# The chain of a chunked RWKV7 recurrence cut from three products a chunk to two, and the tensor engine put into written order

## The chip, the cores and the metric

The kernel runs on one core of one Trainium2 chip. The metric is the device time of one execution in microseconds, lower is better.

The core has a tensor engine (PE) that multiplies, three engines for elementwise work, VectorE (DVE), ScalarE (ACT) and GpSimd (POOL), and SyncE (SP), on whose queue the DMA transfers of this kernel are started. Each runs its own list of instructions in the order of that list, and engines wait for each other by semaphores. Products are accumulated in PSUM, from which VectorE or ScalarE copies them out.

## The reference

One decoder block: a combined input projection, a gated spatial unit (SGU) and an RWKV7 recurrence side by side, an output projection with residual, and cross-attention over 256 memory tokens. Sequence length is 1024, model width 1024; the recurrence has 8 heads of 64. What matters here is the recurrence, a linear one with a state S of 64x64 a head:

```python
def rwkv7_step(state, inp):
    r, w, k, v, a, bb = inp
    sa = jnp.einsum('bhvk,bhk->bhv', state, a)
    state = state * w[:, :, None, :] + sa[..., None] * bb[:, :, None, :] + v[..., None] * k[:, :, None, :]
    y = jnp.einsum('bhvk,bhk->bhv', state, r)
    return state, y
...
h = h + jnp.concatenate([y_sgu, y_rwkv], axis=-1) @ w_out[l]
h = h + mem_cross_attention(h, mem, ln_x_g[l], ln_mem_g[l], w_q[l], w_kv[l], w_o[l])
```

## The kernel before, in words

**Chunks.** The 1024 steps are cut into 16 chunks of 64. Two heads make a pair and share the 128 partitions, so there are 4 pairs, and each pair's sequence is worked in two halves of 8 chunks: 8 halves, counted by n from 0 to 7. Within a chunk the recurrence becomes products. Four masked products of the chunk's factors with each other ("grams"), the inverse of a triangular matrix, and the state of the chunk before give the chunk's output and the next state.

**The stages of a half.**
- `elementwise` (L577 to L636) makes the decay factors. Its products are the decay product (L583, L584), sums (L608) and the bonus (L635).
- `grams` (L656 to L705) makes the grams of each quarter (4 chunks) as 16 products into two PSUM accumulators `co`, empties them with VectorE (L661 to L666), and inverts 16x16 diagonal blocks with VectorE (L673 to L679). The inverse goes through memory (`t_img`, started on SP at L680) and comes back as `t16`.
- `turn` transposes the values and the update factors of a quarter: `avt` (L696, copied by ScalarE at L698) and `bkt` (L702, L703).
- `solve` makes the full 64x64 inverse triangles, `tt`, from the 16x16 blocks in four steps. Each step is one or two batches of 16 products of 64x64 (L717, `pair_mm`) into `cb` or `co`.
- `serial` runs the chunks one after the other. Per chunk it has three products into `us`: `us[0]` applies the factors `ra` to the state (L766); VectorE adds `akv` to one part of it and puts it on the diagonal of `abdiag` (two 64x64 adds, L768); `us[1]` applies the triangle `tt` (L775); ScalarE copies the result into `avt` (L776); `us[2]` makes the state's update (L781), and VectorE adds it to the decayed state, two 64x64 (L787). ScalarE also makes the decayed state (L772) and the chunk's first output part (L778).
- `outputs` (L799, L801) adds the grams' part of the output once per quarter; `finish` normalises a half (L809 to L819, with a power on GpSimd inside `rsqrt_small`, L152 and L153), transposes it (L823) and stores it to `y_scr` (L828).

**Accumulators.** PSUM tiles named `co` exist twice, `cb` once. Decay products, bonus, grams and the transposes of `turn` all use the two `co`.

**Dense work in between.** The input projection, later the output projection, is a long list of dense products. `mm3` issues three products of 128x512 for each step (L177 to L179), since each operand is split into a high and a low part (helper L156, L157; weights are fetched at L161). The function `drive` (L896) runs for n from −2 to 7 and weaves the stages of neighbouring halves: beside the chunks of half n it writes the outputs and end of n − 1, the grams, transposes and solve of n + 1, the elementwise work of n + 2, and 32 or so dense steps. The tables `D_*` give each step a cost and `W_*` a stretch of the half in which its steps are due; `D_HOP` gives the distance between the products of a chunk.

**What sets the order.** The written order is only a proposal in this kernel: a scheduler of the language takes the program and decides each engine's list itself, the tensor engine's included (`with nullcontext():` ahead of the loop over n). Buffers of a rotating tile come free in turn.

Of the kernel before, what the change touches and what calls it, by code (L numbers as in the profile page):

```python
# [18 lines left out]
P = 128  # L19
# [3 lines left out]
C = 64  # L23
# [12 lines left out]
W_S = (0.72, 1.0)  # L36
# [4 lines left out]
D_HOP = (1.2, 0.95, 1.3)  # L41
# [4 lines left out]
D_S = (1.3, 1.3, 2.2, 1.3)  # L46
# [36 lines left out]
def tile_hybrid_block(ctx: ExitStack, tc: tile.TileContext, x, xT, mem, memT, cst_d, vec_d, w_sv, w_blk, w2_d, a2_d,  # L83
# [17 lines left out]
    def cb_ps():  # L101
        return psB.tile([P, 512], F32, name="cb")
# [8 lines left out]
    def cs_(n):  # L111
        o, w = CST[n]
        return cst[:, o:o + w]
# [342 lines left out]
    with tc.tile_pool(name="rw", bufs=1) as rw:  # L456
# [6 lines left out]
        ab_d = [rw.tile([P, P], F32, name=f"abdiag{i}") for i in range(2)]  # L463
        z_buf = [rw.tile([P, NC, C], F32, name=f"zz{i}") for i in range(2)]
        for t in st_d + ab_d + z_buf:
            nc.gpsimd.memset(t, 0.0)
# [240 lines left out]
        def solve(i):  # L707

            u, qs = halves_u[i], quarters[2 * i:2 * i + 2]
            t16 = u["t16"]  # L710
# [30 lines left out]
            u.update(tt=tt, akv=akv)  # L741
            yield

        def serial(i):

            u = halves_u[i]
            ra, dc, tt, akv = u["ra"], u["dc"], u["tt"], u["akv"]
            u["y"] = ytok = rw.tile([P, 4, P], F32, name="ytok", bufs=2)
            for c in range(NC):
# [7 lines left out]
                s_old, s_new, ab = st_d[n % 2], st_d[(n + 1) % 2], ab_d[n % 2]  # L757
                us = psC.tile([P, 3, P], F32, name="us")
                yc = ytok[R[c % 2], c // 2, :]
                if first:  # L760
                    nc.gpsimd.memset(yc, 0.0)
                    for hh in range(2):
                        nc.vector.tensor_copy(out=ab[R[hh], R[hh]], in_=akv[R[hh], c, :])
                else:

                    nc.tensor.matmul(us[:, 0, :], ra[:, c, :, :], s_old, start=True, stop=True)  # L766
                    for hh in range(2):
                        nc.vector.tensor_tensor(out=ab[R[hh], R[hh]], in0=us[R[1], 0, R[hh]], in1=akv[R[hh], c, :],  # L768
                                                op=ALU.add)
# [9 lines left out]
                yield  # L779
                if not last:  # L780
                    nc.tensor.matmul(us[:, 2, :], bkt[:, cq, :], avt[:, cq, :], start=True, stop=True)  # L781
                    for h2 in R:
                        if first:
# [419 lines left out]
```

## Time and profile before

| | us |
|---|---|
| median of 3 runs | 953.71 (952.59 to 954.79) |
| profiled execution | 952.35 |
| its span | 950.6 |
| tensor engine busy | 906.8 (95% of the span) |
| VectorE busy | 593.5 (62%) |
| ScalarE busy | 390.5 (41%) |
| GpSimd busy | 50.5 (5%) |

The span is read in parts. SGU and the first projection lie ahead of 243 us; the recurrence runs from there to 664 us; behind it follow the rest of the output projection and the attention. A "busy" tensor engine may still be filling or draining its pipeline: a dense product shows 0.39 us but the next one starts 0.23 us behind it, so prices are taken from the distance of starts. The chain that ended last goes through the tensor engine for 78% of the span and through VectorE for 13%.

### The profile page before, as it was taken

How to read it: one execution, taken by the hardware profiler on the slowest of the kernel's cores; microseconds unless marked ns; L12 is line 12 of the kernel's file. 1: busy time of each engine (PE TensorE's matmuls, PEld its weight loads, DVE VectorE, ACT ScalarE, POOL GpSimd, SP SyncE). 2: the span in 40 equal slices, each digit the busy share in tenths (PEclk: the TensorE clock that was granted, in tenths of full speed). 3: DMA queues.
4: the chain of work that ended last, by engine and by line, in shares of the span. 5: the costliest groups of instructions: out<-in, count | busy, mean ns of one | idle time of the engine just before them, and what ended most of it. 6: DMA issues, size and time to landing. Idle time of an engine off the chain costs nothing.

```text
span 950.6 us, 16113 instructions
## 1 busy us (share of the span) xinstructions
PE 906.8 (95%) x6236; PEld 728.1 (77%) x6236; DVE 593.5 (62%) x1375; ACT 390.5 (41%) x818; POOL 50.5 (5%) x115
## 2 busy tenths in 40 slices
PE   6989999999999999898989999999799999999996
PEld 6978888888777777676767677677698778888885
DVE  5867233334585878686868789867587664444333
ACT  6763222224442525252616272534266553333222
POOL 0001000012000000000000000000000000000000
PEclk9999999999999999999999999999999999999999
DMA  8862011113122112121111084425462400000001
GB/s 314 264 216 89 23 67 67 67 68 111 40 55 44 37 26 60 26 59 26 48 35 49 24 240 113 115 52 151 143 212 70 136 6 2 26 26 26 26 32 45
DMA packets 86092, 76.86 MB, mean 81 GB/s; under 512 B 38272, under 2 KB 58752, under 8 KB 86016
## 3 DMA queue, kind: packets, MB, share of 16 engines
q1 hardware_dynamic: 84864, 73.73, 24.9%
q10 hardware_dynamic: 1152, 2.10, 0.6%
q8 instruction: 49, 0.80, 0.4%
q14 instruction: 27, 0.22, 0.1%
HBM read 62.17 MB, written 13.64 MB: 80 GB/s over the span
## 4 chain that ended last, share of the span: by engine, by line
PE 78%; DVE 13%; issue 3%; DMA 2%; POOL 2%; ACT 1%; POOLq 0%; SPq 0%; DVEq 0%; ACTq 0%
PE mm L177 21%; PE mm L179 20%; PE mm L178 20%; PE cb L717 3%; PE us L766 2%; PE us L775 2%; PE yps L799 2%; PE us L781 1%; POOL grs L153 1%; DVE gr L666 1%; PE co L717 1%; DVE stdiag L787 1%; DMA w_raw<-in_w_sv 1%; DVE cs L592 1%; PE co L432 1%
## 5 line engine op out<-in xcount | busy, mean ns | idle before, releaser
L177 PE MATMUL mm<-xh,w_hi 128*128 128x512 f32 x400 | 167.2, 418 | 0.0
L179 PE MATMUL mm<-xh,w_lo 128*128 128x512 f32 x400 | 159.8, 400 | 0.0
L178 PE MATMUL mm<-xl,w_hi 128*128 128x512 f32 x400 | 159.5, 399 | 0.0
L157 DVE TENSOR_TENSOR w_lo<-w_raw,w_hi 128x512 fp32r<-128x512 f32 x115 | 78.7, 686 | 63.9 <-ACT w_hi L156 61.4
L156 ACT CAST w_hi<-w_raw 128x512 fp32r<-128x512 f32 x115 | 70.8, 617 | 91.4 <-PE mm L178 75.8
L179 PEld LDWEIGHTS mm<-xh,w_lo 128*128 128x128 f32 x400 | 75.8, 190 | 14.8 <-issue 0.2
L177 PEld LDWEIGHTS mm<-xh,w_hi 128*128 128x128 f32 x400 | 76.0, 190 | 12.9 <-issue 1.0
L178 PEld LDWEIGHTS mm<-xl,w_hi 128*128 128x128 f32 x400 | 76.2, 190 | 12.5 <-issue 0.5
L177 PE MATMUL mm<-wo,w_hi 128*128 128x512 f32 x128 | 54.2, 424 | 0.0
L776 ACT COPY avt<-us 64x128 f32<-64x128 f32 x64 | 16.6, 259 | 90.1 <-PE us L775 89.8
L178 PE MATMUL mm<-wo,w_hi 128*128 128x512 f32 x128 | 52.4, 409 | 0.0
L179 PE MATMUL mm<-wo,w_lo 128*128 128x512 f32 x128 | 51.8, 404 | 0.0
L177 PE MATMUL mm<-vp_h,p_hi 128*128 128x512 f32 x128 | 51.3, 401 | 0.0
L179 PE MATMUL mm<-kp_h,w_lo 128*128 128x512 f32 x128 | 50.1, 391 | 0.0
L177 PE MATMUL mm<-kp_h,w_hi 128*128 128x512 f32 x128 | 50.0, 391 | 0.0
L179 PE MATMUL mm<-vp_h,p_lo 128*128 128x512 f32 x128 | 50.0, 390 | 0.0
L178 PE MATMUL mm<-vp_l,p_hi 128*128 128x512 f32 x128 | 49.9, 390 | 0.0
L178 PE MATMUL mm<-kp_l,w_hi 128*128 128x512 f32 x128 | 49.9, 389 | 0.0
L787 DVE SCALAR_TENSOR_TENSOR stdiag<-us,dc,sd 64x64 f32<-64x64 f32 x112 | 31.6, 283 | 21.9 <-PE us L781 19.4
L772 ACT ACTIVATE sd<-stdiag,dc 128x128 f32<-128x128 f32 x56 | 22.4, 399 | 40.7 <-DVE stdiag L787 37.1
L1040 DVE TENSOR_REDUCE mx<-mm 128x2 f32<-128x512 f32 x16 | 11.1, 691 | 41.8 <-PE mm L179 41.8
L499 ACT ACTIVATE t<-mm,vec 128x512 f32<-128x512 f32 x34 | 23.3, 684 | 33.7 <-PE mm L179 32.7
(272 smaller groups left out, 2029.1 us busy)
## 6 DMA issues: line engine op xcount, KB each, us to landing
w_raw<-in_w_blk SPq DMA_DIRECT2D x50, 256.0 KB, 2.5
w_raw<-y_scr SPq DMA_DIRECT2D x32, 256.0 KB, 3.3
w_raw<-in_w_kv SPq DMA_DIRECT2D x17, 256.0 KB, 3.9
xr<-in_xT SPq DMA_DIRECT2D x8, 512.0 KB, 5.7
w_raw<-in_w_out SPq DMA_DIRECT2D x16, 256.0 KB, 2.8
h_all<-in_x SPq DMA_DIRECT2D x16, 256.0 KB, 4.5
pr<-in_w_qT SPq DMA_DIRECT2D x8, 512.0 KB, 4.4
w_raw<-in_w_o SPq DMA_DIRECT2D x16, 256.0 KB, 2.6
```

What stands on the lines that cost most here:

```text
L156: nc.scalar.copy(out=hi, in_=src)
L157: (eng or nc.vector).tensor_tensor(out=lo, in0=src, in1=hi.bitcast(F32), op=ALU.subtract)
L177: nc.tensor.matmul(ps, lh, rh, start=first, stop=False)
L178: nc.tensor.matmul(ps, lh, rl, start=False, stop=False)
L179: nc.tensor.matmul(ps, ll, rh, start=False, stop=last)
L499: nc.scalar.activation(out=t1[:, 1:HT + 1], in_=ps, func=AF.Copy, scale=vc("mu", b))
L717: nc.tensor.matmul(ps[R[hh], c, :], fl(hh, c), fr(hh, c), start=True, stop=True)
L766: nc.tensor.matmul(us[:, 0, :], ra[:, c, :, :], s_old, start=True, stop=True)
L772: nc.scalar.activation(out=sd, in_=s_old, func=AF.Copy, scale=dcc)
L775: nc.tensor.matmul(us[:, 1, :], tt[:, c - c % 2:c - c % 2 + 2, :], ab, start=True, stop=True)
L787: nc.vector.scalar_tensor_tensor(out=s_new[h2, h2], in0=us[h2, 2, h2], scalar=dcc[h2], in1=sd[h2, h2], op0=ALU.mult, op1=ALU.add)
L799: nc.tensor.matmul(yps[R[c % 2], o:o + 64], gr[:, c, hh, :], avt[:, c, R[hh]], start=True, stop=True)
```

## The change

It has three parts.

**Two products a chunk.** Write A for the `a` part of `ra`, T for the triangle. The three products of a chunk compute T(A S + akv). The new `solve` computes T A and T akv for all 8 chunks of a half ahead of the chain, in a fifth step: A is transposed with the identity (16 products, `at`), T A is made (16 products) and copied by ScalarE over the `a` part of `ra`, T akv is made (16 products) and copied by ScalarE into `avt` in four parts. `serial` is left with `us[0]`, one VectorE add of 64x128 straight into `avt`, and the state's update. The second product, its ScalarE copy and `abdiag` are gone. `tt` and `akv` now have one buffer each instead of two.

**The tables.** `D_HOP` has two entries, `D_S` five; the solve's steps are due from 0.66 instead of 0.72 of a half; the gate of the first outputs of a half goes from 12 to 8 steps, since a chunk has two steps now instead of three.

**The tensor engine's order.** `with nullcontext()` becomes `with tc.manual_schedule(engines={PE})`: the tensor engine's list in the loop over n is the written order. The other engines are still ordered by the scheduler.

```diff
-W_S = (0.72, 1.0)
+W_S = (0.66, 1.0)
-D_HOP = (1.2, 0.95, 1.3)
+D_HOP = (1.0, 1.35)
-D_S = (1.3, 1.3, 2.2, 1.3)
+D_S = (2.2, 1.3, 2.2, 1.3, 2.2)
...
-            t16 = u["t16"]
+            t16, ra = u["t16"], u["ra"]
...
-            tt = rw.tile([P, NC, C], F32, name="tt", bufs=2)
+            tt = rw.tile([P, NC, C], F32, name="tt")
...
-            akv = rw.tile([P, NC, C], F32, name="akv", bufs=2)
+            akv = rw.tile([P, NC, C], F32, name="akv")
+            at = rw.tile([P, NC, C], F32, name="at")
...
+            pa = pair_mm(co_ps(), lambda hh, c: ra[R[hh], c, 1, :], lambda hh, c: ident[R[hh], R[hh]])
+            nc.scalar.copy(out=at, in_=pa)
...
-            u.update(tt=tt, akv=akv)
+            yield
+            ps = pair_mm(cb_ps(), lambda hh, c: at[R[hh], c, :], lambda hh, c: tt[R[hh], c, :])
+            pa = pair_mm(co_ps(), lambda hh, c: tt[R[hh], c, :], lambda hh, c: akv[R[hh], c, :])
+            nc.scalar.copy(out=ra[:, :, 1, :], in_=ps)
+            for j in range(2):
+                for hh in range(2):
+                    nc.scalar.copy(out=qs[j]["avt"][R[0], :, R[hh]], in_=pa[R[hh], QC * j:QC * j + QC, :])
...
-                us = psC.tile([P, 3, P], F32, name="us")
+                us = psC.tile([P, 2, P], F32, name="us")
...
                     nc.tensor.matmul(us[:, 0, :], ra[:, c, :, :], s_old, start=True, stop=True)
-                    for hh in range(2):
-                        nc.vector.tensor_tensor(out=ab[R[hh], R[hh]], in0=us[R[1], 0, R[hh]], in1=akv[R[hh], c, :],
-                                                op=ALU.add)
+                    nc.vector.tensor_tensor(out=avt[R[0], cq, :], in0=us[R[1], 0, :], in1=avt[R[0], cq, :], op=ALU.add)
...
-                nc.tensor.matmul(us[:, 1, :], tt[:, c - c % 2:c - c % 2 + 2, :], ab, start=True, stop=True)
-                nc.scalar.copy(out=avt[R[0], cq, :], in_=us[R[c % 2], 1, :])
...
-                    nc.tensor.matmul(us[:, 2, :], bkt[:, cq, :], avt[:, cq, :], start=True, stop=True)
+                    nc.tensor.matmul(us[:, 1, :], bkt[:, cq, :], avt[:, cq, :], start=True, stop=True)
...
-                    (ok(n), lambda: outputs(2 * n), D_Y, W_Y0, 12),
+                    (ok(n), lambda: outputs(2 * n), D_Y, W_Y0, 8),
...
-        with nullcontext():
+        with tc.manual_schedule(engines={mybir.EngineType.PE}):
```

In the new program most line numbers of the recurrence differ by one: the grams are L655, their evacuations L660 to L665, the bonus L634, the outputs L800 and L802. The chunk's products are `us[0]` at L773 and the update at L780; VectorE's add is L774, the state L786.

**How the order moves, place one: the tensor engine ahead of the first chunk.** From the bonus product to the second quarter's grams of half 0. L177 to L179 are dense products, L656 (L655) grams; `xh`, `xl` are parts of the normalised input. Before:

```order
L635 MATMUL co<-zk,rkb 128x512
L656 MATMUL co<-ra,bk 64x128 x16
L179 MATMUL mm<-xh_99,w_lo 128x512
L177 MATMUL mm<-xh_100,w_hi 128x512
L178 MATMUL mm<-xl_108,w_hi 128x512
L179 MATMUL mm<-xh_100,w_lo 128x512
L177 MATMUL mm<-xh_101,w_hi 128x512
L178 MATMUL mm<-xl_109,w_hi 128x512
L179 MATMUL mm<-xh_101,w_lo 128x512
L656 MATMUL co<-ra,bk 64x128 x16
```

After:

```order
L634 MATMUL co<-zk,rkb 128x512
L177 MATMUL mm<-xh_99,w_hi 128x512
L178 MATMUL mm<-xl_107,w_hi 128x512
L179 MATMUL mm<-xh_99,w_lo 128x512
L655 MATMUL co<-ra,bk 64x128 x16
L177 MATMUL mm<-xh_100,w_hi 128x512
L178 MATMUL mm<-xl_108,w_hi 128x512
L179 MATMUL mm<-xh_100,w_lo 128x512
L655 MATMUL co<-ra,bk 64x128 x16
```

Seven dense products stood between the first and the second grams, three stand there now. From the decay product to the second grams it is 57 dense products before and 30 after.

**Place two: the tensor engine where one half ends and the next begins.** From the last outputs of a half (L799, L800) to the next application of the factors to the state. Before:

```order
L799 MATMUL yps<-avt,gr 64x64 x6
L656 MATMUL co<-ra,bk 64x128 x16
L775 MATMUL us<-abdiag_1926,tt 128x128
L177 MATMUL mm<-xh_100,w_hi 128x512
L178 MATMUL mm<-xl_108,w_hi 128x512
L179 MATMUL mm<-xh_100,w_lo 128x512
L177 MATMUL mm<-xh_101,w_hi 128x512
L781 MATMUL us<-avt,bkt 128x128
L178 MATMUL mm<-xl_109,w_hi 128x512
L179 MATMUL mm<-xh_101,w_lo 128x512
L656 MATMUL co<-ra,bk 64x128 x16
```

After:

```order
L800 MATMUL yps<-avt,gr 64x64 x8
L655 MATMUL co<-ra,bk 64x128 x16
L780 MATMUL us<-avt,bkt 128x128
L655 MATMUL co<-ra,bk 64x128 x16
L177 MATMUL mm<-xh_100,w_hi 128x512
L178 MATMUL mm<-xl_108,w_hi 128x512
L179 MATMUL mm<-xh_100,w_lo 128x512
```

Two chunk products and six dense products stood between the two batches of grams; one chunk product stands there now.

**Place three: VectorE at the same place, in the new program.** L802 to L820 are the end of the old half, L660 to L665 the evacuations of the grams, L786 the state.

```order
L802 TENSOR_TENSOR ytok<-ytok,yps 128x256
L810 TENSOR_REDUCE gsm<-ytok 128x8
L811 SCALAR_TENSOR_TENSOR ytok<-gsm,ytok 128x512
L660 TENSOR_TENSOR an<-co,cst 128x256
L662 TENSOR_TENSOR nt_5822<-co,cst 64x256
L663 TENSOR_TENSOR ak_5823<-co,cst 64x256
L665 TENSOR_TENSOR gr<-co,cst 128x4x64
L786 SCALAR_TENSOR_TENSOR stdiag_1925<-us,dc,sd 64x64 x2
L665 TENSOR_TENSOR gr<-co,cst 128x4x64
L816 TENSOR_REDUCE gsv<-ysq 128x8
L152 TENSOR_SCALAR rs_t<-gsv 128x8
L820 TENSOR_TENSOR ytok<-ytok,grs 128x512
```

Before it is the same list but for one move: both evacuations into `gr` stand ahead of the state's update there, and here the second one stands behind it.

## Rows read from the trace of the kernel before

**Rows 1.** Windows: us, busy time and instructions of each engine, PEclk, DMA.
```profile
243.00:664.00 421.00, 401.27 (x3628) 302.54 (x3627) 326.43 (x903) 178.98 (x411) 21.59 (x58) 0.99 0.24 66
449.00:452.40 3.40, 3.40 (x10) 2.73 (x9) 2.63 (x8) 0.98 (x2) 0.37 (x2) 0.50 0.21 19
497.00:503.00 6.00, 5.77 (x32) 4.52 (x33) 3.24 (x11) 2.72 (x8) 0.37 (x2) 1.00 0.17 22
684.25:687.65 3.40, 3.25 (x11) 2.70 (x12) 2.43 (x4) 1.52 (x3) 0.00 (x0) 0.54 1.02 334
```

**Rows 2.** Waits of the tensor engine, 243 to 690 us: total, times, longest.
```profile
PE us L775 <- DVE abdiag L768: 8.6, 4, 2.3
...
PE us L766 <- DVE stdiag L787: 4.4, 8, 1.0
...
PE us L781 <- ACT avt L776: 1.5, 2, 0.7
```

**Rows 3.** Timeline of the tensor engine: start, us, operation.
```profile
427.87 1.15 PE L717 MATMUL cb<-zz,tt 64*64 64x64 f32 x32
428.95 0.49 PE L766 MATMUL us<-stdiag,ra 128*128 128x128 f32 x2
429.19 0.47 PE L177 MATMUL mm<-xh,w_hi 128*128 128x512 f32 x1
429.51 0.39 PE L178 MATMUL mm<-xl,w_hi 128*128 128x512 f32 x1
429.74 0.40 PE L179 MATMUL mm<-xh,w_lo 128*128 128x512 f32 x1
```

**Rows 4.** Timeline of three engines, from the decay product to the second grams.
```profile
242.94 0.40 PE L583 MATMUL co<-lstk,whi 128*128 128x512 f32 x1
...
246.31 0.63 ACT L596 ACTIVATE th<-kk 128x512 f32<-128x512 f32 x1 [1.33 <-DVE cs L592]
...
255.67 0.69 DVE L633 TENSOR_TENSOR zk<-zr,zk 128x512 f32<-128x512 f32 x1
...
257.03 1.02 PE L635 MATMUL co<-zk,rkb 128*128 128x512 f32 x2
...
262.02 0.73 PE L656 MATMUL co<-ra,bk 64*64 64x128 f32 x13 [0.16 <-DVE gr L666]
```

**Rows 5.** Timeline of VectorE, the first half's inverse triangles.
```profile
271.17 0.60 DVE L673 TENSOR_TENSOR nt<-ak,cst 64x256 f32<-64x256 f32 x1
...
284.52 0.17 DVE L679 TENSOR_TENSOR nt<-nt,xtmp 64x14 f32<-64x14 f32 x1
...
291.54 0.71 DVE L725 STREAM_TRANSPOSE tt<-t 128x512 f32<-128x512 f32 x1 [5.40 <-DMA t<-t_img]
```

**Rows 6.** Timeline, boundary at 437 us; the last row one half later.
```profile
437.06 0.42 DVE L801 TENSOR_TENSOR ytok<-ytok,yps 128x256 f32<-128x256 f32 x1
...
440.18 0.76 DVE L666 TENSOR_TENSOR gr<-co,cst 128x256 f32<-128x256 f32 x2
440.85 0.57 DVE L787 SCALAR_TENSOR_TENSOR stdiag<-us,dc,sd 64x64 f32<-64x64 f32 x2
...
444.10 0.69 DVE L819 TENSOR_TENSOR ytok<-ytok,grs 128x512 f32<-128x512 f32 x1 [1.75 <-POOL grs L153]
...
440.89 1.19 PE L656 MATMUL co<-ra,bk 64*64 64x128 f32 x32
...
447.34 0.49 PE L775 MATMUL us<-abdiag,tt 128*128 128x128 f32 x2 [2.31 <-DVE abdiag L768]
...
497.23 0.38 PE L775 MATMUL us<-abdiag,tt 128*128 128x128 f32 x1 [2.31 <-DVE abdiag L768]
```

**Rows 7.** Timeline behind the last chunk: tensor engine and SP's queue.
```profile
663.94 0.38 PE L766 MATMUL us<-stdiag,ra 128*128 128x128 f32 x2
...
679.39 0.37 SPq L958 DMA_DIRECT2D pr<-in_w_qT  x1
...
684.25 0.35 PE L177 MATMUL mm<-ktt,p_hi 128*128 128x256 f32 x1 [4.97 <-DMA w_raw<-y_scr]
```

More of the change, by code (lines that the diff above doesn't have):

```diff
@@ L462, in tile_hybrid_block @@
         st_d = [rw.tile([P, P], F32, name=f"stdiag{i}") for i in range(2)]
-        ab_d = [rw.tile([P, P], F32, name=f"abdiag{i}") for i in range(2)]
         z_buf = [rw.tile([P, NC, C], F32, name=f"zz{i}") for i in range(2)]
-        for t in st_d + ab_d + z_buf:
+        for t in st_d + z_buf:
             nc.gpsimd.memset(t, 0.0)
@@ L746, in serial @@
             u = halves_u[i]
-            ra, dc, tt, akv = u["ra"], u["dc"], u["tt"], u["akv"]
+            ra, dc = u["ra"], u["dc"]
             u["y"] = ytok = rw.tile([P, 4, P], F32, name="ytok", bufs=2)
@@ L761, in serial @@
                     nc.gpsimd.memset(yc, 0.0)
-                    for hh in range(2):
-                        nc.vector.tensor_copy(out=ab[R[hh], R[hh]], in_=akv[R[hh], c, :])
                 else:
                     nc.tensor.matmul(us[:, 0, :], ra[:, c, :, :], s_old, start=True, stop=True)
-                    for hh in range(2):
-                        nc.vector.tensor_tensor(out=ab[R[hh], R[hh]], in0=us[R[1], 0, R[hh]], in1=akv[R[hh], c, :],
-                                                op=ALU.add)
+                    nc.vector.tensor_tensor(out=avt[R[0], cq, :], in0=us[R[1], 0, :], in1=avt[R[0], cq, :], op=ALU.add)
                     if not last:
@@ L773, in serial @@
                 yield
-                nc.tensor.matmul(us[:, 1, :], tt[:, c - c % 2:c - c % 2 + 2, :], ab, start=True, stop=True)
-                nc.scalar.copy(out=avt[R[0], cq, :], in_=us[R[c % 2], 1, :])
+                if not last:
+                    nc.tensor.matmul(us[:, 1, :], bkt[:, cq, :], avt[:, cq, :], start=True, stop=True)
+                    for h2 in R:
+                        if first:
+                            nc.vector.tensor_scalar(out=s_new[h2, h2], in0=us[h2, 1, h2], scalar1=dcc[h2],
+                                                    scalar2=None, op0=ALU.mult)
+                        else:
+                            nc.vector.scalar_tensor_tensor(out=s_new[h2, h2], in0=us[h2, 1, h2], scalar=dcc[h2],
+                                                           in1=sd[h2, h2], op0=ALU.mult, op1=ALU.add)
                 if not first:
                     nc.scalar.copy(out=yc, in_=us[R[0], 0, :])
-                yield
-                if not last:
-                    nc.tensor.matmul(us[:, 2, :], bkt[:, cq, :], avt[:, cq, :], start=True, stop=True)
-                    for h2 in R:
-                        if first:
-                            nc.vector.tensor_scalar(out=s_new[h2, h2], in0=us[h2, 2, h2], scalar1=dcc[h2],
-                                                    scalar2=None, op0=ALU.mult)
-                        else:
-                            nc.vector.scalar_tensor_tensor(out=s_new[h2, h2], in0=us[h2, 2, h2], scalar=dcc[h2],
-                                                           in1=sd[h2, h2], op0=ALU.mult, op1=ALU.add)
                 yield
@@ L900, in drive @@
                          for j, (_, d, lo, hi, _) in enumerate(others) for i, c in enumerate(d))
-            pace = 0.97 * total / (max(n_steps, 1) / 3 * (sum(D_HOP) + 3 * D_STEP))
+            pace = 0.97 * total / (max(n_steps, 1) / 2 * (sum(D_HOP) + 2 * D_STEP))
             t = ready = goal = 0.0
@@ L907, in drive @@
                     t += D_STEP
-                    goal += pace * (D_HOP[k % 3] + D_STEP)
-                    ready = max(goal, t + D_HOP[k % 3])
+                    goal += pace * (D_HOP[k % 2] + D_STEP)
+                    ready = max(goal, t + D_HOP[k % 2])
                     k += 1
@@ L934, in tile_hybrid_block @@
                 steps = serial(n) if ok(n) else none
-                drive(steps, 3 * NC if ok(n) else 0, others, n_dense.get(n, 32))
+                drive(steps, 2 * NC if ok(n) else 0, others, n_dense.get(n, 32))
                 for g, *_ in others:
```

2 lines of the change are left out of this document (1 added, 1 removed).

## The prediction

> **What bounds the kernel now.** I read the windows first [rows 1]. From 243 us, where the recurrence phase begins, to 664 us, where its last chunk product starts, the tensor engine is busy 401.27 of 421.00 us, at a mean granted clock of 0.99. VectorE is busy 326 us and ScalarE 179 us of the same stretch. So the phase is bound by tensor-engine work, and only 421.00 − 401.27 = 19.7 us of it is idle. The second row is a stretch with the clock at 0.50 (1.2 GHz). There are two such in the phase, each 3.4 us long and behind a 2.3-us idle of the engine (447.34 in [rows 6] is one of the two). Half speed costs half of the stretch, 1.7 us, so 3.4 us for both. A third idle of that size, at 497.23 [rows 6], is followed by a clock of 1.00 [rows 1].
>
> The waits view [rows 2] names the idle time that the change aims at: the three recurrence products wait 8.6 us for the diagonal add (4 times), 4.4 us for the new state and 1.5 us for ScalarE's copy, 14.5 us in all. The time that a shorter chain can give back is therefore 14.5 us at the very most. The latency of the chain is already covered, since the scheduler fills it with dense products.
>
> Behind the phase stands one more wait: the tensor engine stands 4.97 us at 684.25 until the last y_scr data have come back [rows 7].
>
> **Work that goes and work that comes.** The price rows [rows 3] are starts on one engine, so their differences are pitches: 16 pair products in 32 parts 428.95 − 427.87 = 1.08 us; a dense product 429.74 − 429.51 = 0.23; a chunk product 0.24, and the dense product behind it 0.32 instead of 0.23, so some 0.33 when it is cut in between others, 0.24 when it is not. I take 0.27.
> Added: three batches of 16 pair products in each of 8 halves, 24 × 1.08 = +25.9 us.
> Removed: one of three chunk products, 64 × 0.27 = −17.3 us.
> The written order also keeps small products together (runs of outputs 32 to 15, grams 22 to 16, transposes 47 to 39, pair products 54 to 39), 46 changes fewer at about 0.2 (0.1 for each side, from 0.32 against 0.23), −9.2 us.
> Sum −0.6 us: the tensor engine's work stays what it was. Bounds: +9 if a change of kind costs nothing, −6 if a chunk product costs 0.33 and a change 0.23. On ScalarE 64 copies go and six per half come, off the path except where said below. VectorE changes two 64x64 adds for one of 64x128 per chunk and needs no more time.
> What can move the time is then idle time. What there was, 19.7 us, is replaced as a whole by what the written order gives, stage by stage. No row of before shows a tensor engine that may not step over a waiting instruction, so I walk the new order along the chains as the trace dates them.
>
> **The first half, before any chunk runs.** The chain to the grams is decay product at 242.94, tanh 246.31, factors up to 255.67 on VectorE, bonus product 257.03, second grams 262.02 [rows 4]. In before 57 dense products stand between the first and the last of these, and the engine waits under 1 us. In the new order 30 stand there. The chain is as long as it was, so 27 × 0.233 = 6.3 us become idle. Then the inversion: its VectorE part starts at 271.17, ends at 284.52, and the triangle comes back through memory for the transpose at 291.54 [rows 5]; the pair products that need the triangle as it arrives start 1.5 us before that, at 290.0. In the new order the engine reaches these, with the 6.3 us counted, at about 287.3: 2.7 us more. With the 2.0 us that stood here in before and 1 us for the new step (its products want ScalarE's copy of the transposed a; an allowance, with no row): **12 us**.
>
> **The half of pair 0, chunks 0 to 7.** Here the second grams come right behind the first ones, and both accumulators must be emptied: 1.8 us by the sum of the next paragraph, with less queued on VectorE. The triangle needs 291.54 − 262.02 = 29.5 us from second grams to transpose [rows 4, 5], and 31.3 in this half; the work in the new order between the two is 26.4 us by the pitches plus 1.8 idle: 3 us. The four new copies to avt hold one of the two accumulators, but lie beside dense products. **4.7 us.**
>
> **The six steady halves.** This is the largest term and rests on the boundary at 437 us [rows 6]. There VectorE does the end of one half (sum, centring, variance, scale: 437.06 to 444.10 and 0.69) and the evacuation of both grams of the next, in one queue, and the chunk's add stands behind all of it: the chunk product waits until 447.34. That is 447.34 − 437.06 = 10.3 us for one chunk step. It includes 1.75 us in which VectorE itself waits for GpSimd's power [rows 6]. In before the tensor engine fills this with 7.4 us of work that the scheduler pulled in, and waits 2.9 us (2.31 of it in one place).
> VectorE's queue holds the same operations in the new program (only the abdiag adds change), so the 10.3 us stand. The tensor engine's written order in them is grams 1.1, chunk product 0.27, grams 1.1, three dense products 0.8, state product 0.3, nine dense 2.1: 5.7 us, up to 6.0 with cuts. So 4.3 us idle, in two places: the second grams directly behind the first must wait for the last evacuation of the first ones, and that one now stands behind the state update (0.57 us in before's row), about 2.9 us; the second chunk product waits for the rest, 1.4 us.
> Then per half 0.5 us where a pair of transposes waits for its accumulator with no dense product between, and 0 to 1 us where the new triangle's arrival and the written order tie: 0.9. Each half 5.2 us, six **31.2 us**. Bounds: 2.9 per half if the grams' wait overlaps all of the rest, 7 if GpSimd answers later or if the single tt and akv buffers hold the solve back.
> The last half has no grams and no solve: **1 us**.
>
> **Behind the last chunk.** 22 dense products less stand ahead of the last state product in the new order, −5.1 us to its start; they are done behind it. From that product to the products of the next part it is 684.25 − 663.94 = 20.3 us in before [rows 7], a chain of outputs, normalisation, transposes, store and load. In the new order 18 dense products (4.2 us) instead of 6 and a chunk product (1.7) stand ahead of the outputs: +2.5 us to the store. The load of the next weights is queued behind the store on SP in both (679.39), so nothing covers that: **+2.6 us** with one cut. If the chain's waits shrink as VectorE is freer, 0; if the 22 products all push it, +5.
>
> **Sum.** Work to the last state product: 421.00 − 19.7 − 3.4 = 397.9, − 5.1 − 0.6 = 392.2. Idle 12 + 4.7 + 31.2 + 1 = 48.9. Clock: of the three idles of 2.3 us in before two brought a slow stretch, and the 4.97 us at 684.25 brought one as well (0.54 behind it) [rows 1, 7]. The new program has nine gaps of that size or more (two in the first half, one in pair 0's, six boundaries); at two of three that is six stretches, 6 × 1.7 = 10.2 us. 243 + 392.2 + 48.9 + 10.2 = 694.3 against 663.94: +30.4. With the tail +33.0. The profiled execution took 952.35 us (its span 950.6), so 985.4; the median of the runs lies 1.4 above it: **987 us**.
>
> **Rivals.**
> *Faster, because the chain really is the limit.* If the two accumulators come free before the second grams want them (VectorE running the evacuations ahead of the normalisation, as the scheduler is free to do), nothing new waits and the 14.5 us of [rows 2] go: 953.7 − 14.5 + 0 to 2.6, about 940. It decides when VectorE's chain from outputs to second evacuation falls from 10.3 to under 6 us. Against it: VectorE's built order has the normalisation and the state update ahead of that evacuation, and GpSimd's answer in between.
> *Only the ends lose.* If in the steady halves idle and clock stay at before's rate, the first half's loss (6.3 + 2.7) and the tail's 2.6 remain: 953.7 + 11.6, about 965. For it: planner distances that fit 10 us; against it: 5.7 us of work there by count.
> *The clock drops at each gap.* If each of the nine gaps brings its stretch, and the boundaries, which have two gaps each, some a second one, that is 9 to 12 stretches in place of six, +5 to +10: about 994. For it: the new gaps are longer than those that fell two times in three. Against it: the third case, and that a second gap 2 us behind the first may fall into a stretch that is slow already. If on the other side only two fall as now, 980.
> [...]
> *No difference.* Idle and slow clock together cost 19.7 + 3.4 = 23.1 us now. With the first half's 12, 4.5 us less work ahead of the last product spent again behind it, and the tail's wait, each of seven halves could idle some 1.5 us; the count above gives three times that.
> That the change does not do what it says I rule out by the built order: the third product and its ScalarE copy are gone.
>
> **How the numbers follow.** Forecast 0.60 (974 to 996), only the ends 0.16, the clock at each gap 0.08, faster 0.10, no difference 0.06. The last two, 0.16, and little else lie below 960; 1000 holds most of the clock's rival and the upper bounds of the work. So the range is 960 to 1000. A measurement of this kernel can tell about 0.2%, 2 us, from no change. Faster by more than that 0.10, within it 0.06, slower 0.84.
>
> **What would show it.** In the profile after: tensor-engine busy time from 243 us to the last state product near 394 us, with idle near 49; a wait of the second grams for VectorE's evacuation of some 3 us in each of six halves; waits for the diagonal gone, but a wait of the state product for avt at the boundaries; the first chunk product some 9 us late; the end 2 to 3 us longer. Wrong would be: grams that do not wait (VectorE's queue is not the limit), idle in every chunk (the planner's spacing is too tight for the new chain), or a clock of 1.00 throughout (the gaps cost only themselves). Right would be about one slow stretch in two of three halves.

## The result, and the profile after

The changed kernel takes 982.70 us (median of 4 runs, 979.73 to 991.97) against 954.25 us before (four runs; 953.71 was the median of the first three): 1.0308 times as long, with an interval of 1.0280 to 1.0336. The forecast was 987 us, slower, in a range from 960 to 1000. The profiled execution's span is 983.1 us, 32.5 us more than before's 950.6; the prediction's sum was +33.0.

The four executions differ in the mean granted clock of their whole span, 0.966 in the profiled one, then 0.974, 0.980 and 0.959, and the lower it is, the longer they take (984.83, 980.57, 979.73 and 991.97 us); the clock's share below is that of the profiled one.

That the totals agree does not say that the terms do, so each is measured here. First the same cut as in [rows 1]: a window from the first decay product of the phase to the last state product, then nine windows inside it (the first half up to the first chunk, the half of pair 0, the boundaries of the six others, the last half). The columns are length, busy time of each engine, granted clock, DMA.

```profile
243.77:692.67 448.90, 403.87 (x4235) 319.97 (x4234) 314.55 (x829) 183.17 (x391) 21.81 (x58) 0.94 0.22 59
...
243.80:306.50 62.70, 54.39 (x541) 41.03 (x539) 36.95 (x86) 23.63 (x42) 2.00 (x11) 0.92 0.14 37
306.50:353.00 46.50, 44.00 (x501) 34.80 (x502) 34.16 (x95) 20.38 (x45) 1.70 (x7) 1.00 0.15 38
353.00:402.00 49.00, 43.71 (x498) 34.65 (x490) 35.45 (x98) 19.82 (x43) 3.08 (x9) 1.00 0.17 42
402.00:453.00 51.00, 47.36 (x521) 38.01 (x520) 37.30 (x101) 21.65 (x48) 3.27 (x8) 0.93 0.16 40
453.00:505.00 52.00, 48.46 (x525) 38.46 (x524) 35.97 (x99) 21.27 (x48) 3.07 (x9) 0.93 0.16 39
505.00:557.00 52.00, 47.75 (x522) 38.36 (x522) 36.87 (x100) 21.35 (x47) 3.27 (x8) 0.93 0.14 35
557.00:614.00 57.00, 48.17 (x515) 38.04 (x513) 42.15 (x110) 25.35 (x55) 2.15 (x4) 0.91 0.51 151
614.00:647.00 33.00, 29.49 (x211) 23.40 (x209) 27.98 (x81) 13.24 (x31) 1.64 (x1) 0.90 0.32 83
647.00:692.80 45.80, 40.64 (x426) 33.33 (x427) 27.86 (x61) 16.59 (x39) 1.64 (x1) 0.93 0.26 72
```

The tensor engine is busy 403.87 us, nearly what it was (401.27, [rows 1]), but idle for 448.90 − 403.87 = 45.0 us instead of 19.7, and at a mean clock of 0.94 instead of 0.99. Part of the busy time is slow: nine stretches at 1.2 GHz (granted clock 0.50), some 55 us long in all with some 48 us of busy time in them, cost half of that busy time, 24.1 us. At full speed the work is 379.8 us.

The waits of the tensor engine in the same window (total, times, longest), beside [rows 2]:

```profile
PE co L655 <- DVE gr L665: 17.6, 15, 2.3
PE cb L717 <- DMA t<-t_img: 11.9, 9, 4.9
PE co L701 <- ACT th L585: 5.0, 7, 0.9
PE co L634 <- DVE zk L632: 2.6, 1, 2.6
PE us L780 <- DVE avt L774: 1.9, 2, 1.3
```

The 14.5 us for the diagonal, the state and the ScalarE copy are gone but for 1.9. What came are the second grams, waiting for VectorE to empty their accumulators, and the pair products, waiting for the triangle. One boundary, tensor engine and then VectorE, beside [rows 6]:

```profile
402.75 1.22 PE L655 MATMUL co<-ra,bk 64*64 64x128 f32 x32
403.89 0.49 PE L780 MATMUL us<-avt,bkt 128*128 128x128 f32 x2
406.62 0.61 PE L655 MATMUL co<-ra,bk 64*64 64x128 f32 x2 [2.24 <-DVE gr L665]
407.47 0.49 PE L655 MATMUL co<-ra,bk 64*64 64x128 f32 x4 [0.24 <-DVE gr L665]
```
```profile
404.10 0.69 DVE L811 SCALAR_TENSOR_TENSOR ytok<-gsm,ytok 128x512 f32<-128x512 f32 x1
404.71 0.42 DVE L660 TENSOR_TENSOR an<-co,cst 128x256 f32<-128x256 f32 x1
...
406.05 0.42 DVE L665 TENSOR_TENSOR gr<-co,cst 128x256 f32<-128x256 f32 x1
406.39 0.57 DVE L783 TENSOR_SCALAR stdiag<-us,dc 64x64 f32<-64x64 f32 x2
406.99 0.42 DVE L665 TENSOR_TENSOR gr<-co,cst 128x256 f32<-128x256 f32 x1
```

The evacuations of the first grams stand in VectorE's list behind the centring of the old half (404.10 and 0.69) and begin when it is done. The second grams start when the first accumulator is empty, at 406.05 and 0.42, and stop again until the other one is, behind the state update: 2.24 and 0.24 us of idle. Six boundaries have such a gap of 2.23 to 2.28 us.

The slow stretches follow these gaps. Windows of the changed kernel; the clock is the third column from the end:

```profile
356.50:363.30 6.80, 5.05 (x49) 3.78 (x50) 4.39 (x11) 0.56 (x2) 1.64 (x1) 1.00 0.16 32
406.60:413.40 6.80, 6.54 (x43) 5.05 (x44) 4.46 (x12) 0.40 (x1) 1.64 (x1) 0.51 0.17 36
457.80:464.70 6.90, 6.19 (x42) 4.81 (x43) 4.95 (x13) 0.56 (x2) 1.64 (x1) 0.51 0.15 32
509.00:515.90 6.90, 6.22 (x42) 4.84 (x43) 4.92 (x13) 0.40 (x1) 1.64 (x1) 0.51 0.16 33
563.60:567.00 3.40, 3.40 (x18) 2.63 (x12) 1.65 (x4) 0.00 (x0) 1.64 (x1) 0.51 0.03 5
618.20:625.10 6.90, 6.11 (x41) 4.77 (x42) 4.92 (x14) 1.02 (x2) 1.64 (x1) 0.51 0.15 31
```

Of the six gaps four are followed by a stretch of 6.8 to 6.9 us, one by 3.4 us, and one, at 356.4 us, by none. The engine is busy 28.5 us in the five, so they cost 14.2 us, beside 13.5 us for the six gaps themselves. The other four of the nine stretches lie in the first half (two) and at the waits for the triangle of 3.20 and 4.87 us in halves 5 and 6 (two).

Behind the last chunk, beside [rows 7]: the tensor engine, then two windows, from the last state product to the end of the span, before and after.

```profile
692.67 0.38 PE L773 MATMUL us<-stdiag,ra 128*128 128x128 f32 x2
...
697.09 0.73 PE L800 MATMUL yps<-avt,gr 128*64 128x64 f32 x16
...
706.78 1.09 PE L824 MATMUL yps<-cst,ytok 128*128 128x128 f32 x4 [5.82 <-DVE ytok L820]
```
```profile
663.94:950.60 286.66, 273.08 (x1343) 226.25 (x1341) 145.42 (x262) 113.59 (x238) 13.33 (x17) 0.99 0.19 63
692.67:983.10 290.43, 277.64 (x1375) 230.59 (x1373) 149.80 (x268) 116.59 (x242) 13.33 (x17) 0.98 0.21 67
```

The wait has changed its place: the last transposes now stand 5.82 us for the normalisation, and the reload of y_scr, which cost 4.97 us [rows 7], is covered by the dense products behind them. From the last state product to the end of the span it is 290.43 us, 3.8 more than before's 286.66. Idle there is 12.8 us instead of 13.6, so the 3.8 us are work, the dense products that stood ahead of the last state product before.

So the 32.5 us are 0.8 ahead of the phase, 27.9 in it and 3.8 behind it; and the 27.9 are 25.3 more idle, 20.7 more slow clock and 18.1 less work at full speed.

### The profile page after: what moved, and what is told of

Its sections match the earlier page's. It is cut to its first block, busy times and chain, and to the rows that moved or that the text cites. A ratio compares the mean times of both kernels' runs of the same rounds, so it can differ in the third digit from the quotient of the medians.

```text
span 983.1 us, 17313 instructions
## 1 busy us (share of the span) xinstructions
PE 914.4 (93%) x6876; PEld 750.5 (76%) x6876; DVE 586.2 (60%) x1307; ACT 397.6 (40%) x802; POOL 50.1 (5%) x113
## 4 chain that ended last, share of the span: by engine, by line
PE 71%; DVE 14%; DMA 6%; issue 3%; ACT 3%; SPq 1%; POOL 1%; POOLq 0%; DVEq 0%; ACTq 0%
PE mm L177 19%; PE mm L179 18%; PE mm L178 18%; PE cb L717 4%; PE co L717 2%; DMA t<-t_img 2%; DMA t_img<-nt 2%; PE co L655 1%; SPq L683 1%; PE us L773 1%; DVE w_lo L157 1%; DVE xtmp L676 1%; DVE stdiag L786 1%; DVE nt L678 1%; PE co L634 1%
## 5 line engine op out<-in xcount | busy, mean ns | idle before, releaser
L177 PE MATMUL mm<-xh,w_hi 128*128 128x512 f32 x400 | 171.6, 429 | 0.0
L179 PE MATMUL mm<-xh,w_lo 128*128 128x512 f32 x400 | 159.5, 399 | 0.0
L179 PEld LDWEIGHTS mm<-xh,w_lo 128*128 128x128 f32 x400 | 77.1, 193 | 17.2
L177 PEld LDWEIGHTS mm<-xh,w_hi 128*128 128x128 f32 x400 | 77.8, 194 | 15.5 <-issue 2.7
L178 PEld LDWEIGHTS mm<-xl,w_hi 128*128 128x128 f32 x400 | 77.8, 195 | 12.8 <-issue 0.8
L177 PE MATMUL mm<-wo,w_hi 128*128 128x512 f32 x128 | 55.4, 433 | 0.0
L179 PE MATMUL mm<-wo,w_lo 128*128 128x512 f32 x128 | 51.5, 403 | 1.0 <-DVE w_lo L157 1.0
L177 PE MATMUL mm<-vp_h,p_hi 128*128 128x512 f32 x128 | 51.3, 401 | 0.0
L179 PE MATMUL mm<-kp_h,w_lo 128*128 128x512 f32 x128 | 50.1, 391 | 0.0
L177 PE MATMUL mm<-kp_h,w_hi 128*128 128x512 f32 x128 | 50.0, 391 | 0.0
L179 PE MATMUL mm<-vp_h,p_lo 128*128 128x512 f32 x128 | 50.0, 390 | 0.0
L789 ACT COPY ytok<-us 64x128 f32<-64x128 f32 x60 | 15.4, 257 | 83.3 <-DVE stdiag L786 76.7
L655 PE MATMUL co<-ra,bk 64*64 64x128 f32 x512 | 26.0, 314 | 18.0 <-DVE gr L665 17.6
L786 DVE SCALAR_TENSOR_TENSOR stdiag<-us,dc,sd 64x64 f32<-64x64 f32 x112 | 31.7, 283 | 15.3 <-PE us L780 12.9
L655 PEld LDWEIGHTS co<-ra,bk 64*64 64x64 f32 x512 | 19.0, 154 | 23.9 <-issue 18.3
```

The source lines that it names most:

```text
L177: nc.tensor.matmul(ps, lh, rh, start=first, stop=False)
L178: nc.tensor.matmul(ps, lh, rl, start=False, stop=False)
L179: nc.tensor.matmul(ps, ll, rh, start=False, stop=last)
L655: nc.tensor.matmul(pss[hh][R[x], c, :, :], bk[R[hh], cc, x, :], ra[R[hh], cc, :, :], start=True, stop=True)
L786: nc.vector.scalar_tensor_tensor(out=s_new[h2, h2], in0=us[h2, 1, h2], scalar=dcc[h2], in1=sd[h2, h2], op0=ALU.mult, op1=ALU.add)
```

## The experiments

**The written order, or the two products? (e1_sched, e2_before_written)** The change does two things at once, so each was made alone. The changed kernel with the scheduler:

```diff
-        with tc.manual_schedule(engines={mybir.EngineType.PE}):
+        with nullcontext():
```

> The changed kernel, but the tensor engine's list is left to the scheduler as in the kernel before. My theory (the loss is the written order, not the two-product chain): the gaps of 2.2 us at the half boundaries and the slow clock behind them go, the dense products fill them again; work is a few us more than in the written order (more changes of kind), so 940 to 958 us, idle of the tensor engine in the recurrence under 20 us and at most two slow stretches. Rival (the longer solve, ScalarE's copies and the single tt and akv buffers cost the time): 970 us or more.

Measured: 956.44 us against 955.72 for before beside it, ratio 1.0007 (0.9987 to 1.0026). No difference, and inside the theory's 940 to 958. The kernel before with the same line turned the other way:

> The kernel before with its three products a chunk, but with the tensor engine in written order. Theory: the same boundary, so the same gaps and clock, and one more chain wait a chunk: 980 to 1010 us. Rival (the written order costs only together with the new tables and the new solve): within 1% of before, 945 to 963 us.

Measured: 985.17 us, ratio 1.0318 (1.0280 to 1.0355), as slow as the changed kernel. The windows of the two, from decay product to last state product, and e2's largest waits:

```profile
243.70:666.50 422.80, 414.64 (x4252) 316.33 (x4251) 314.17 (x835) 184.93 (x396) 20.97 (x58) 1.00 0.25 66
```
```profile
245.40:694.60 449.20, 394.35 (x3621) 309.67 (x3619) 331.32 (x903) 179.87 (x411) 20.73 (x58) 0.96 0.23 62
...
PE co L656 <- DVE gr L666: 15.7, 10, 2.3
PE us L766 <- DVE stdiag L787: 14.5, 17, 1.7
PE us L775 <- DVE abdiag L768: 10.2, 14, 2.5
```

| us, in the phase | idle | slow clock costs | work at full speed | sum |
|---|---|---|---|---|
| before: scheduler, three products | 19.7 | 3.4 | 397.9 | 421.0 |
| e1: scheduler, two products | 8.2 | 0 | 414.6 | 422.8 |
| e2: written order, three products | 54.9 | 16.4 | 377.9 | 449.2 |
| after: written order, two products | 45.0 | 24.1 | 379.8 | 448.9 |

Each row is one execution. Read downwards in pairs, the two products do what they should to the waits (idle −11.5 with the scheduler, −9.9 without). Under the scheduler work grows by 16.7 us and eats it: 26.9 us of pair products come, 13.7 of chunk products go, the grams, cut oftener, take 31.8 us instead of 22.4, and the other kinds take 5.9 less. In the written order work grows by only 1.9. The written order takes 20 to 35 us of work away (some 3.8 of it, with two products, 15 dense products that go behind the last chunk, 879 in e1 and 864 in the changed kernel) and adds 35 to 37 us of idle and 13 to 24 us of slow clock. The loss is the written order's, with either chain. The theory's numbers for e1's idle and clock hold too (under 20 us, no slow stretch); its "a few us more" of work are 34.8.

**The gap at the grams, first try. (e3_grams_apart, e4_grams_far)** One table entry, so that dense products stand between the two batches:

```diff
-W_G = (0.0, 0.13)
+W_G = (0.0, 0.26)
```

> The changed kernel with one table entry changed, W_G from (0, 0.13) to (0, 0.26): at a half boundary six dense products stand between the first and the second grams where none stood. Theory: six gaps of 2.24 us shrink to under 1 us, and with them go most of the five or six slow stretches of 6.8 us (about 3 us each): 20 to 27 us less than the changed kernel, 956 to 963 us. Rival (VectorE's chain is as long as it was, so the wait moves to the next chunk product): the same time within 5 us, 977 to 986 us. If gaps under 1 us bring slow stretches as well: only the idle is saved, 970 to 975 us.

Measured: 995.98 us, ratio 1.0412 (1.0372 to 1.0452), slower than the changed kernel: a miss, and not the rival's either. The further one, (0, 0.40):

> As the one above with W_G (0, 0.40): first grams three dense products and a chunk product later, second grams behind 21 dense products and two chunk products. Theory: no gap at the grams at all, but the inversion starts some 6 us later, so the solve waits for the triangle coming back through memory in each half, 3 to 4 us each where it was about 1: 960 to 980 us, slower than the run with 0.26. Rival (the triangle has slack): the fastest of the written orders, under 956 us.

Measured: 1025.47 us, ratio 1.0725 (1.0704 to 1.0747): slower than e3, as the theory said, but far above its 960 to 980. The largest waits of e3, then of e4:

```profile
PE cb L717 <- DMA t<-t_img: 26.9, 20, 7.5
PE us L773 <- ACT ytok L789: 13.9, 14, 1.4
```
```profile
PE cb L717 <- DMA t<-t_img: 55.9, 20, 9.0
PE us L773 <- ACT ytok L789: 11.1, 12, 1.5
```

The wait for the accumulators is gone from both, but the triangle has no slack. From the first grams to the load of the triangle it is 435.62 − 402.75 = 32.9 us at the changed kernel's boundary shown above and 33.2 at e3's, by these rows (SP's queue of the changed kernel, then e3's first grams and its SP queue):

```profile
435.62 3.00 SPq L683 DMA_DIRECT2D t<-t_img  x4
```
```profile
409.14 1.20 PE L655 MATMUL co<-ra,bk 64*64 64x128 f32 x32
...
442.36 2.58 SPq L683 DMA_DIRECT2D t<-t_img  x4
```

The tensor engine, with the dense products laid under the gap, is sooner at the pair products and stands there: 4.95 us ahead of the first chunk, 6.21 and 7.52 in halves 5 and 6, where the changed kernel stands 0.95, 3.20 and 4.87. A second wait comes up that hardly was there before (0.5 us): a chunk product stands for ScalarE's copy of the output part, since there is one buffer `us`. The gap's cause can't be read from these two runs, as in both the triangle's chain then sets the time.

**The gap at the grams, second try. (e5_grams_banks)** The order stays; the second grams get two accumulators that nobody uses at that time, so the triangle is not moved:

```diff
-                pss = [co_ps().rearrange("p (c x t) -> p c x t", c=QC, x=2) for _ in range(2)]
+                pss = [t.rearrange("p (c x t) -> p c x t", c=QC, x=2)
+                       for t in ((co_ps(), co_ps()) if j == 0 else (cb_ps(), psC.tile([P, 512], F32, name="yps")))]
```

> The changed kernel, written order unchanged, but the second grams of a half write into two other accumulators, cb and yps, which nobody uses then, so they have nothing to wait for. Theory (the boundary gap comes from the two co accumulators): the six gaps of 2.24 us go without moving the triangle, VectorE can empty the second grams while it waits for GpSimd, and most of the 6.8-us slow stretches behind the gaps go with them, 10 to 15 us of slow clock; a wait of 1 to 2 us may come up at the next chunk product. 955 to 966 us. Rival (VectorE's chain of 10.3 us at the boundary is the limit, wherever the wait shows): 977 to 985 us. If the gaps go and the slow stretches stay: 968 to 974 us.

Measured: 963.45 us, ratio 1.0078 (1.0057 to 1.0100), inside the theory's 955 to 966. About three quarters of the loss are gone: 1.0308 − 1.0078 = 0.023 of 955 us, 22 us. Its window in the phase, then the boundary:

```profile
243.30:668.30 425.00, 388.41 (x4236) 306.99 (x4235) 314.17 (x829) 183.86 (x392) 21.16 (x58) 0.94 0.23 63
```
```profile
396.84 0.49 PE L781 MATMUL us<-avt,bkt 128*128 128x128 f32 x2
397.26 0.32 PE L656 MATMUL cb<-ra,bk 64*64 64x128 f32 x1
...
400.02 0.46 PE L774 MATMUL us<-stdiag,ra 128*128 128x128 f32 x2 [0.73 <-DVE stdiag L784]
```

The second grams follow the chunk product at once, and the next state product waits 0.73 us: the rival, that VectorE's chain sets the time wherever the wait shows, falls. The triangle comes sooner too, 424.18 − 395.66 = 28.5 us behind the first grams:

```profile
395.66 1.25 PE L656 MATMUL co<-ra,bk 64*64 64x128 f32 x32
...
424.18 2.72 SPq L684 DMA_DIRECT2D t<-t_img  x4
```

Idle in the phase is 36.6 us, 8.4 less than in the changed kernel; slow clock costs 7.2 (four stretches, 17 us), 16.9 less; work is 1.4 more. Idle falls by less than the 13.5 us of the gaps, since other waits grow: for the triangle in halves 5 and 6 to 4.17 and 6.36 us, and of chunk products for ScalarE's copy, as in e3, from 0.5 to 6.6 us. (The clock column reads 0.95 through most of this one execution, outside the four stretches, while the products stand 0.23 us apart as elsewhere; the four are counted by 0.5.)

**The first half, and the tail. (e6_prologue, e7_tail)** On top of e5, dense steps were moved, first to the first half:

```diff
-        n_dense = {-2: 16, 5: 16 + N_PROJ[0], 6: N_PROJ[1], 7: N_PROJ[2]}
+        n_dense = {-2: 25, 5: 7 + N_PROJ[0], 6: N_PROJ[1], 7: N_PROJ[2]}
```

> As the one above, and nine dense steps (27 products) moved from the half n = 5 to n = -2, where the chain to the first grams runs. Theory (the 6.3 us of the prediction's first-half term): the gaps ahead of the sums, the bonus and the second grams, 6.4 us in the changed kernel, and their slow clock, 4.7 us, go; half 5, which already waits for its triangle, may give back 2 us. 6 to 10 us less than the run above. Rival (the dense products only delay the chain, the first chunk starts later by what they take): the same time as above or 3 us more.

Measured: 963.99 us, ratio 1.0082 (1.0052 to 1.0112): no gain, the rival's. Of the gaps ahead of the first grams only one of 1.61 us is over 0.9, but half 5 then lacked the nine steps: its wait for the triangle grew from 4.17 to 5.48 us, a chunk product waited 3.39, and slow clock cost 13.2 instead of 7.2.

Then six steps from ahead of the last outputs to behind them:

```diff
-... 7: N_PROJ[2]}
+... 7: N_PROJ[2] - 6}
...
-            weave([..., (finish(halves_u[-1]), 3, 0.1, 0.5), (dense, 8, 0.0, 1.0)])
+            weave([..., (finish(halves_u[-1]), 3, 0.05, 1.1), (dense, 14, 0.0, 1.0)])
```

> As the one above, and six dense steps (18 products) that stood between the last state product and the last outputs now stand behind these outputs, with the last transposes 39 products behind the outputs instead of 9. Theory (the chain behind the last chunk is what counts): the 5.8-us wait of the last transposes goes, the store starts 3 to 4 us earlier, and a wait of under 2 us for the reload may come up: 3 to 6 us less than the run above. Rival (the wait only moves behind the store, to the reload of y_scr): within 1.5 us of the run above.

Measured: 961.75 us, ratio 1.0076 (1.0051 to 1.0101), not to be told from e6. The tail's waits in e6, then in e7 (the largest), and a row of VectorE in e7:

```profile
PE yps L825 <- DVE ytok L821: 6.1, 1, 6.1
```
```profile
PE mm L177 <- issue: 2.5, 1, 2.5
```
```profile
681.88 0.69 DVE L955 TENSOR_TENSOR w_raw<-w_raw,mbc 128x512 f32<-128x512 f32 x1 [1.15 <-DMA w_raw<-kv_scr]
```

The wait of the transposes is gone and a smaller one stands ahead of the products of the next part, but the end did not move by what was expected. The edit did less than was expected of it: 12 of the 18 dense products still stand between the last state product and the outputs. And what the transposes gained was lost behind them: they start 12.6 us behind the last state product instead of 14.3, but the store starts 17.6 us behind it, where it was 17.8. In e7 a step of the next stage stands in VectorE's list ahead of the last two multiplications and waits 1.15 us for its load.

**Spreading the rest. (e9_rebalanced_half, e10_rebalanced_five)** What is left in e7 are mostly waits for the triangle in halves 5 and 6, so dense steps were spread over the last three halves anew, 27, 33, 21 and 30, 30, 21 instead of 21, 28, 30, with 12 steps in the last weave:

```diff
-        n_dense = {-2: 25, 5: 7 + N_PROJ[0], 6: N_PROJ[1], 7: N_PROJ[2] - 6}
+        n_dense = {-2: 25, 5: 27, 6: 33, 7: 21}
```

> As the run with the tail changed, with dense steps spread anew over the last halves: 27, 33 and 21 (21, 28 and 30 there), 12 of the last ones woven in behind the last outputs. Theory (what is left of the loss is the triangle's latency in halves 5 and 6, waits of 6.2 and 6.0 us and 3.9 us at a chunk product, with slow clock behind them): six dense steps more in half 5 and five in half 6 cover some 6 to 8 us of that and 4 us of slow clock, half 7 loses 2 to 3: 950 to 955 us, faster than the kernel before by up to 0.5%. Rival (dense work is conserved, so what covers one latency uncovers another): 958 to 965 us.

Measured: 968.47 us, ratio 1.0140 (1.0111 to 1.0169).

> As the one above with 30, 30 and 21 steps: half 5 as long as in the changed kernel. Theory: the wait in half 5 goes as a whole, that in half 6 stays at 5 us; 951 to 956 us. Rival: 958 to 965 us.

Measured: 961.53 us, ratio 1.0077 (1.0049 to 1.0104). The second is the rival's, and the first is slower than either forecast: e9's triangle still cost 11.1 us, and half 7 and the tail, with less to do, show waits of 3.8 and 3.6 us that weren't there. The dense work is a fixed amount; laid under one latency it is missing under the next.

**Each order where it is good. (e11_mixed, e12_written_chunks)** On top of e5, the written order holds only in a part of the loop:

```diff
-        with tc.manual_schedule(engines={mybir.EngineType.PE}):
-            for n in range(-2, NH):
+        with nullcontext():
+            for n in range(-2, NH):
+                with tc.manual_schedule(engines={mybir.EngineType.PE}) if 0 <= n < 5 else nullcontext():
```

> The changed kernel with the second grams in two other accumulators (e5), and the tensor engine in written order only in the halves 0 to 4; ahead of the first chunk, in the halves 5 to 7 and behind the last chunk the scheduler orders it. Theory (written order saves changes of kind where dense work covers the chains, and loses where a latency must be filled: the first half, the triangles of halves 5 and 6, the tail): against e5's 963.5 the first half gives back 6 us and 3 us of slow clock, the late halves 10 us of waits and 5 of slow clock, the tail 3, and about 8 us of work come back in changes of kind: 943 to 950 us, faster than the kernel before. Rival (dense work is conserved; the scheduler fills early and lacks later): 955 to 962 us.

Measured: 948.93 us, ratio 0.9932 (0.9911 to 0.9954): faster than the kernel before, by 0.5 to 0.9%. With `0 <= n` instead:

> As the one above, with written order in all eight halves of chunks; the scheduler orders only what is ahead of the first chunk's half and behind the last chunk. Theory: the first half and the tail give back about 9 us in all against e5, the waits for the triangle in halves 5 and 6 stay: 953 to 957 us. Rival: as e5, 961 to 966 us.

Measured: 966.62 us, ratio 1.0111 (1.0090 to 1.0133): the rival's, as e5 or a little worse (its range ended at 966). e11's window in the phase and its largest waits:

```profile
243.20:661.40 418.20, 399.21 (x4252) 311.96 (x4251) 317.44 (x835) 185.92 (x396) 22.28 (x58) 0.99 0.25 67
```
```profile
PE us L774 <- ACT ytok L790: 4.1, 8, 1.1
PE cb L718 <- DMA t<-t_img: 3.7, 5, 2.3
```

Idle 19.0, slow clock 4.1 (one stretch), work 395.1. Between the two runs only the halves 5 to 7 differ, and they make 1.0111 − 0.9932, 17 us. There, with the triangle's way through memory longer than the half's dense work in its written place, the scheduler fills the gap: e12's waits for the triangle of 4.20 and 6.37 us in halves 5 and 6 are gone in e11. Ahead of the first chunk and behind the last one the scheduler brought nothing that can be measured (e12 against e5). That the written order in halves 0 to 4 makes e11 faster than e1 is not shown, only likely: e11 has 19.5 us less work in the phase than e1 with as many products in it, but no run has the scheduler throughout with e5's accumulators, and e1's idle is 8.2 us where the two runs lie 7 us apart.

## Why the prediction was right, point by point

**Direction, place and size.** +33.0 was forecast and 32.5 measured. The reason given, the written order's gaps at the boundaries, is shown by e2 (the same loss without the new chain) and e5 (most of it gone without a change in the order). That the sizes agree to 0.5 us is luck: two terms were off by 12 and 14 us in opposite directions, as shown below.

**Idle time, term by term.**

| us of idle | forecast | measured |
|---|---|---|
| first half, up to the first chunk | 12 | 8.3 |
| half of pair 0 | 4.7 | 2.5 |
| six steady halves with their solves | 31.2 | 33.9 |
| last half | 1 | 0.3 |
| sum | 48.9 | 45.0 |

(The wait of 4.87 us at 651 us, in the last window, belongs to half 6's solve and is counted there.) In the six halves the gap at the second grams was put at 2.9 us and was 2.24 and 0.24. The rest was put at the chunk product, 1.4, and lies elsewhere too: that product waits only twice, and the triangle, for which 0 to 1 us a half was allowed, takes 3.20 and 4.87 us in halves 5 and 6. There the dense work of the planner is 30 and 28 steps instead of 32, which the walk didn't look at half by half.

**The first half.** 9 us later was forecast for the first chunk's product; its update product starts at 306.5 instead of 301.9, of which 0.8 come from ahead. The 6.3 us of missing dense products were right (four gaps of 1.58, 1.11, 2.61 and 1.09), but the 2.7 us on top, from adding the triangle's latency to it, were not: the pair products waited 0.95 and 0.30 us. Nor were the 2.0 us taken over from before: up to its first update product the engine is idle 0.8 us there (58.06 of 58.90 us busy from 243.00). The 1 us for the new step stood on a misreading. The transposes of A stand in the solve's first step and not, as said in the section on the change, in the fifth; their copy is made at 295.0, the product that reads it starts at 301.7, and nothing waits for it.

**Work, the first mis-sized term.** −0.6 was forecast; 397.9 − 5.1 and 379.8 give −13.0. By starts in the two traces, at full speed: pair products 45.7 to 68.9 us (+23.2, forecast +25.9), chunk products 42.7 to 28.8 (−13.9, forecast −17.3), grams and outputs 36.7 to 29.3 (−7.4), dense products 0.267 us each before and 0.251 after, 216.8 us for 864 of them where 0.267 would make 231 (−14). The last two were the step "46 changes fewer at about 0.2", −9.2, and are −21. It counted only four kinds of change, and the cut groups themselves became faster too: grams fell from 22.4 to 19.5, outputs from 14.3 to 9.8.

**The clock, the second.** 10.2 us were forecast (six stretches of 3.4 us), 24.1 measured in the profiled execution (nine, most of 6.8 us). The count was put at two of three gaps and was five of six at the boundaries; two stretches came at the triangle's waits, which were not among the nine gaps counted. But above all the length was taken from before's two, of 3.4 us each. The two errors, +12.4 in work and −13.9 in clock, cancel, which the forecast had no reason to expect. The rival "the clock drops at each gap" was the nearer one in its mechanism, and its price was too small by the same step.
The Trainium skill ("TensorE: Matmul & The Clock Gate", section "HAM oscillation — how this bites in real kernels") describes a kernel in which a wait for a transfer, longer than the gaps at the boundaries here, stands between bursts of products and each burst starts at the slow clock again. Here the same came behind gaps of 2.23 to 2.28 us, at five boundaries of six.

**The tail.** +2.6 forecast, +3.8 measured, but not by the path named. The 18 dense products do stand ahead of the outputs (697.09 − 692.67 = 4.4 us, where 4.2 was said), but the wait at the reload, which was to pass this on to the end, is gone, and idle behind the last state product is 0.8 us less than before. What came is work: the 22 dense products that the forecast had moved behind the last chunk and taken for covered there, its upper bound of 5.

**The rivals.** *Faster, because the chain is the limit*: e1 takes the chain's waits away (idle 8.2 us) and is no faster, since the added work costs as much. *Only the ends lose*: 33.9 of the 45.0 us of idle lie in the six steady halves, and e12 and e6 show that the ends alone give nothing back. *No difference* was the scheduler's version of the same change.

**What stays open.** Why the gap at 356 us brought no slow stretch and the others stretches of 3.4 or 6.8 us, the same gap before the same products, is not settled. Nor is why the gaps in e2 were mostly followed by 3.4 us and those of the changed kernel by 6.8. As the four executions of the changed kernel differ in their granted clock, it may differ from one execution to the next; only one of each was profiled.

## What to carry to other kernels

A scheduler's order and a written one fail differently: the first cuts long runs of products into short ones and pays for each cut, the second stands still wherever a latency was not written around. Compare the two halves of that account (work at full speed; idle and the slow clock behind it) stage by stage, and try each where it wins; the fastest run here, e11, is such a mix.
Before a wait is filled by moving products, look for the resource that they wait for. Two free accumulators took away the gap that other positions in the order only turned into another wait.
A gap of 2 us in a dense stretch of tensor-engine work should be priced at what the clock makes of it, not at its own length: on top came 1.7 to 3.3 us at five gaps here and nothing at the sixth, 2.4 us on average.

## What the runs showed of the hardware that I had not expected

An idle of 2.24 us between small products was followed, at four boundaries of six, by 6.8 us of the tensor engine at 1.2 GHz, twice as long as the stretches behind gaps of the same size in the kernel before: a cost of about 3 us behind a gap of 2.2.

A dense product's mean distance to the next start depends on how often it is cut: 0.267 us where a scheduler mixed kinds freely, 0.251 in the written order, 0.228 inside a long run. Over some 870 products that is as much as the whole chain's waits, 14 us.
